# Decay rows and gate rows of a DeltaNet layer spread over the partitions by DMA from DRAM instead of by transpositions

## The chip, the cores and the metric

The kernel runs on one core of one Trainium2 chip. The metric is the device time of one launch in microseconds (us), the median of several runs. The engines are TensorE (PE; PEld is its weight load), VectorE (DVE), ScalarE (ACT), GpSimd (POOL) and SyncE (SP); each runs its own queue of instructions in order. DMAs are issued from a queue of an engine, here SP's and POOL's.

## The reference

One decoder layer on 256 rows of 2048 float32 values, with a conditioning vector c: a modulation (six vectors of 2048, among them the gates ga1 and ga2), a gated DeltaNet with 16 query/key heads and 32 value heads of 128, and a SwiGLU of width 5632, each followed by a residual sum and a layer norm.

```python
mod = (silu(c) @ mod_w + mod_b)              # sh1, sc1, ga1, sh2, sc2, ga2
h   = x * (1 + sc1) + sh1
qkv, z, b, a = split(h @ w_in)               # conv of 4 taps and silu on qkv
beta, g = sigmoid(b), -exp(a_log) * softplus(a + dt_bias)
gc    = cumsum(g)                            # within a chunk, per value head
decay = where(i >= j, exp(gc[i] - gc[j]), 0)
L     = where(i > j, beta[i] * (k[i] . k[j]) * decay, 0)
u, w  = solve(I + L, [v * beta, k * beta * exp(gc)])
o     = chunk by chunk: q*exp(gc) @ state + (where(i>=j, q.k * decay)) @ (u - w @ state)
x = layer_norm(alpha * x + ga1 * (gated_norm(o, z) @ w_out))
x = layer_norm(alpha * x + ga2 * ((silu(h2 @ w_gate) * (h2 @ w_up)) @ w_down))
```

So `gc` is used twice per head, once along the rows (a value per partition) and once along the columns of a matrix (the same row of 128 values in every partition). The gates ga1 and ga2 multiply along the columns too: the same row of 2048 values in every partition.

## The kernel before

The large matrix products (w_in, w_out, w_gate/w_up, w_down) take almost all of PE's time. Weights stream from DRAM in blocks of 512 KB (`raw`), issued by SP. ACT rounds each block to the reduced type of PE (`wh`, L190), DVE subtracts to get the rest (`wl`, L191), and each product is three matmuls (hi x wh, hi x wl, lo x wh; L223 to L225) of 128x128 by 128x512. I call these the main matmuls. `raw`, `wh` and `wl` have four buffers each, one block serves 12 main matmuls.

The work of the DeltaNet is laid between the main matmuls of w_in (and, at its end, of other products). The code is written as small generators with a due time in units of 24 main matmuls; `advance` runs those that are due as the main products are written, `at(p)` gives them that priority, and `yield d` puts the rest of a task d units later. So constants such as LA1, LA2 and LA3 set where an instruction stands among the main matmuls. The engines then run what stands in their queue, in order.

The 32 value heads are worked in four groups q of 8, one stretch of the program each. Once at the start of the DeltaNet `gates` (L410) makes beta, gc, its negative ngc and others, as columns: one value per partition (position in a chunk of 128), one column per chunk and head. In each stretch there are four tasks `la_task` (two chunks c by two halves g of four heads). A task makes `dg`, gc of four heads added to a mask `below` of -1e30 (L543, ACT, Identity with bias), transposes the four matrices on PE into a PSUM tile `gd` (L547), takes Exp of it with bias ngc into `dm` (L551, ACT), multiplies keys with keys and queries on PE into another `gd` tile `pk` (L556), and multiplies `pk` with `dm` on DVE into `LA` (L561). `gd` has two buffers in PSUM; `dg` and `dm` share the tag `V` of three buffers with tiles of `state_task`. `solve_task` then starts by reading the diagonal blocks of `LA`, and `state_task` follows (its last product is V times LA, L685). At its end come a power on POOL for the output norm (`fo`, L718), a product on DVE (L719) and the multiplication with z (L795). Inverse norms `rn` of keys and queries are POOL powers too (L509), read on DVE (`rr`).

The gate rows: `gate_row` makes, for ga1 and ga2, a tile of 128 x 2048 by 16 transposes of a column repeated 128 times (L838) and four ACT copies (L839); `residual` reads it (L845) after the first column group of w_out and of w_down.

Of the kernel before, what the change touches and what calls it, by code (L numbers as in the profile page):

```python
# [8 lines left out]
F32 = mybir.dt.float32  # L9
F32R = mybir.dt.float32r  # L10
I32 = mybir.dt.int32
AF = mybir.ActivationFunctionType
OP = mybir.AluOpType
# [3 lines left out]
D = 2048  # L17
S = 256
KT = D // 128
# [10 lines left out]
def gdn_layer_kernel(ctx: ExitStack, tc: tile.TileContext, x, c, mod_w, mod_b, ln_g, ln_b,  # L30
                     w_gu, w_down, w_in, conv_w, a_log, dt_bias, norm_w, w_out, out):
    nc = tc.nc
# [2 lines left out]
    SPLIT, MOD0, MODEVERY = 10, 30.0, 0.95  # L35
    MGAP, CGAP0, CGAP, CSTEP = 1.5, 1.0, 2.0, 2.3
    CONV, PAIR, SILU = 0.2, 0.4, 2.4
    GDN, LAGAP, LA1, LA2, LA3, SOLVE, HOP = 3.0, 0.5, 0.3, 0.6, 1.5, 5.4, 0.6
    ALONE, MACW, ZW, OW = 1.5, 1.0, 0.1, 0.3


    consts = ctx.enter_context(tc.tile_pool(name="consts", bufs=1))
    work = ctx.enter_context(tc.tile_pool(name="work", bufs=2))
# [3 lines left out]
    dram = ctx.enter_context(tc.tile_pool(name="dram", bufs=2, space=DRAM))  # L47

    act = nc.scalar.activation
    tt = nc.vector.tensor_tensor  # L50
    ts = nc.vector.tensor_scalar
    stt = nc.vector.scalar_tensor_tensor
    mm = nc.tensor.matmul
    tr = nc.tensor.transpose
# [35 lines left out]
    def tp():  # L90
        return psum.tile([128, 512], F32, name="tp", tag="tp", bufs=2)

    def gd():
        return psum.tile([128, 512], F32, name="gd", tag="gd", bufs=2)
# [17 lines left out]
    jp = work.tile([128, 128], I32, name="jp", tag="hf", bufs=2)  # L112
    nc.gpsimd.iota(jp, pattern=[[1, 128]], base=0, channel_multiplier=-1)
    ident = consts.tile([128, 128], F32, name="ident")
# [3 lines left out]
    ones = upper[:, 127:128]  # L118
    mhalf = consts.tile([128, 16], F32, name="mhalf")
    nc.vector.memset(mhalf, -0.5)  # L120
    below = consts.tile([128, 128], F32, name="below")
    ts(below, jp, 0.0, -1e30, op0=OP.is_gt, op1=OP.mult)

    pbit = work.tile([128, 1], I32, name="pbit", tag="gw0", bufs=1)
    nc.gpsimd.iota(pbit, pattern=[[0, 1]], base=0, channel_multiplier=1)
# [7 lines left out]
    p = tp()  # L133
# [16 lines left out]
    p = tp()  # L150
# [244 lines left out]
    gp = gp_ctx.__enter__()  # L395
# [6 lines left out]
    gc = consts.tile([128, 2, 32], F32, name="gc")  # L402
    ngc = consts.tile([128, 2, 32], F32, name="ngc")
    egc = consts.tile([128, 32], F32, name="egc")
    negc = consts.tile([128, 32], F32, name="negc")
    XN = gp.tile([64, 16, 64], F32, name="XN", tag="XN", bufs=1)
    nc.gpsimd.memset(XN[0:32, :, 32:64], 0.0)
    kse = consts.tile([128, 32], F32, name="kse")

    def gates(ps):  # L410
        bT = work.tile([128, 256], F32, name="bT", tag="hf", bufs=2)
        act(bT[64:128, :], ps[64:128, 0:256], AF.Copy)
        p = tp()
        for t in range(2):
            tr(p[:, t * 64:(t + 1) * 64], bT[64:128, t * 128:(t + 1) * 128], ident[64:128, 64:128])
        ba = work.tile([128, 2, 64], F32, name="ba", tag="hf", bufs=2)
        nc.vector.tensor_copy(ba, p[:, 0:128].rearrange("p (a b) -> p a b", a=2))
        nA = work.tile([128, 32], F32, name="nA", tag="gw0", bufs=1)
        act(nA, alogB, AF.Exp)
        e = work.tile([128, 2, 32], F32, name="e", tag="gw1", bufs=1)  # L420
        act(e, ba[:, :, 0:32], AF.Exp, scale=-1.0)
        ts(e, e, 1.0, None, op0=OP.add)
        nc.vector.reciprocal(beta, e)
        xa = work.tile([128, 2, 32], F32, name="xa", tag="gw2", bufs=1)
        tt(xa, ba[:, :, 32:64], dtB[:, None, :].to_broadcast([128, 2, 32]), op=OP.add)
        ab = work.tile([128, 2, 32], F32, name="ab", tag="gw3", bufs=1)
        stt(ab, xa, -1.0, xa, op0=OP.mult, op1=OP.max)
        en = work.tile([128, 2, 32], F32, name="en", tag="gw1", bufs=1)
        act(en, ab, AF.Exp, scale=-1.0)
        s = work.tile([128, 2, 32], F32, name="s", tag="gw3", bufs=1)  # L430
        ts(s, en, 2.0, None, op0=OP.add)
        nc.vector.reciprocal(s, s)
        tt(s, s, en, op=OP.mult)
        s2 = work.tile([128, 2, 32], F32, name="s2", tag="gw1", bufs=1)
        tt(s2, s, s, op=OP.mult)
        q = work.tile([128, 2, 32], F32, name="q", tag="gw4", bufs=1)
        ts(q, s2, 1.0 / 15.0, None, op0=OP.mult)
        for n in (13, 11, 9, 7, 5, 3):
            stt(q, q, 1.0 / n, s2, op0=OP.add, op1=OP.mult)
        stt(q, q, 1.0, s, op0=OP.add, op1=OP.mult)  # L440
        ts(xa, xa, 0.0, None, op0=OP.max)
        stt(q, q, 2.0, xa, op0=OP.mult, op1=OP.add)
        stt(q, q, -1.0, nA[:, None, :].to_broadcast([128, 2, 32]), op0=OP.mult, op1=OP.mult)
        p = tp()
        mm(p[:, 0:64], upper, q.rearrange("p a b -> p (a b)"), start=True, stop=True)
        mm(p[:, 64:96], ones.to_broadcast([128, 128]), q[:, 0, :], start=True, stop=True)
        nc.vector.tensor_copy(gc, p[:, 0:64].rearrange("p (a b) -> p a b", a=2))
        ts(ngc, gc, -1.0, None, op0=OP.mult)
        act(egc, gc[:, 1, :], AF.Exp)
        ts(negc, egc, -1.0, None, op0=OP.mult)  # L450
        tt(kse, p[:, 64:96], gc[:, 0, :], op=OP.subtract)
        act(kse, kse, AF.Exp)
# [83 lines left out]
    def la_task(q, c, g, sc):  # L536

        kqq, hv, la = kq[q], q * 8, LA[q]
        s0 = c * 8 + g * 4
        dg = gp.tile([128, 4, 128], F32, name="dg", tag="V", bufs=3)  # L540
        for i in range(4):
            h = hv + g * 4 + i
            act(dg[:, i, :], below, AF.Identity, bias=gc[:, c, h:h + 1])  # L543
        yield LA1
        pb = gd()
        for i in range(4):
            tr(pb[:, i * 128:(i + 1) * 128], dg[:, i, :], ident)  # L547
        dm = gp.tile([128, 4, 128], F32, name="dm", tag="V", bufs=3)
        for i in range(4):
            h = hv + g * 4 + i  # L550
            act(dm[:, i, :], pb[:, i * 128:(i + 1) * 128], AF.Exp, bias=ngc[:, c, h:h + 1])  # L551
        yield LA2
        pk = gd()
        for n in range(2):
            nn = g * 2 + n
            mm(pk[:, n * 256:(n + 1) * 256], kqq[:, nn, 0, c * 128:(c + 1) * 128],  # L556
               kqq[:, nn, :, c * 128:(c + 1) * 128], start=True, stop=True)
        for i in range(4):
            h = g * 4 + i
            src = pk[:, (i // 2) * 256:(i // 2 + 1) * 256].rearrange("p (a b) -> p a b", a=2)  # L560
            stt(la[:, s0 + i], src, sc[:, 0, c, h:h + 1], dm[:, i, None, :].to_broadcast([128, 2, 128]),  # L561
                op0=OP.mult, op1=OP.mult)
# [268 lines left out]
    def gate_row(tag, cols, name):  # L831

        row = held.tile([128, D], F32, name=name, tag=tag)
        for g in range(4):
            p = tp()
            for i in range(4):
                k = 4 * g + i
                tr(p[:, i * 128:(i + 1) * 128], cols[:, k:k + 1].to_broadcast([128, 128]), ident)  # L838
            act(row[:, g * 512:(g + 1) * 512], p, AF.Copy)  # L839
        return row  # L840

    def residual(row, g, t, ps, xin, st):
# [157 lines left out]
    with at(n0 + 16):  # L1000
        for src, op in ((ln_g, OP.mult), (ln_b, OP.add)):
            row = held.tile([128, D], F32, name="lrow", tag="h2")
# [16 lines left out]
    with tc.tile_pool(name="ph3", bufs=1, reuse_waits="tile") as p3:  # L1019
# [67 lines left out]
        for g in range(4):  # L1087
            if g == 1:
                for i, src in enumerate((ln_g, ln_b)):
                    for gg in range(4):  # L1090
                        tag, n = ("sg", 2) if i and gg > 1 else ("an", 6)
# [32 lines left out]
```

## Time and profile before

| what | value |
|---|---|
| median of 3 runs | 1725.81 us (1724.95 to 1726.1) |
| profiled execution | 1724.8 us, its span 1723.0 us, mean PE clock 0.992 |
| busy PE, PEld | 1668.4 us (97%), 1325.3 us (77%) |
| busy DVE, ACT, POOL | 1140.0 us (66%), 879.3 us (51%), 49.0 us (3%) |
| chain that ended last | PE 71%, DVE 11%, DMA 8%, issue 5%, ACT 3% |

The span is the time from the first to the last instruction of the profiled execution. The chain is the work that ended last, followed back to what released each step. The mean duration of an instruction includes time in which its predecessor still runs in the pipeline; the step between two starts is the cost on a full engine.

### The profile page before, as it was taken

Reading aid. Unit: us, or ns where it says so; the run is one execution under the profiler, and the core shown is the slowest. Engines: PE = TensorE matmul, PEld = TensorE weight load, DVE = VectorE, ACT = ScalarE, POOL = GpSimd, SP = SyncE. Lnnn points to the kernel's source line nnn. Section 1 sums busy time; section 2 is a strip of 40 time slices with the busy share of each in tenths; the row PEclk is TensorE's granted clock in tenths of the full one; section 3 lists DMA queues with packets and bytes.
Section 4 is the critical chain, followed back from the end, with each engine's and each line's share of the span. In section 5 each row is a group of like instructions: output and inputs, shape, how many; then the busy total and the mean of one; then the engine's idle time right before and its main releaser. Section 6 shows DMA issues by size and latency. Waiting matters only on the chain.

```text
span 1723.0 us, 23257 instructions
## 1 busy us (share of the span) xinstructions
PE 1668.4 (97%) x8685; PEld 1325.3 (77%) x8685; DVE 1140.0 (66%) x1641; ACT 879.3 (51%) x1426; POOL 49.0 (3%) x58
## 2 busy tenths in 40 slices
PE   5999999999999999999999999999999999999996
PEld 2666777787887878787788778888878887888885
DVE  2466988958966988847776865764567444455455
ACT  2433669769568667564333734444444443433331
POOL 0000000001001000000000000000000000000000
PEclk8999999999999999999999999999999999999998
DMA  9998785535863777747888576886678666765653
GB/s 351 364 337 282 225 290 186 171 111 160 257 205 112 245 247 240 247 147 237 300 285 278 159 259 193 298 271 188 187 243 290 186 190 204 249 195 190 196 193 107
DMA packets 183938, 390.82 MB, mean 227 GB/s; under 512 B 12096, under 2 KB 14320, under 8 KB 182800
## 3 DMA queue, kind: packets, MB, share of 16 engines
q1 hardware_dynamic: 181808, 378.64, 67.5%
q0 software_dynamic: 2016, 10.68, 1.8%
q8 instruction: 68, 1.11, 0.3%
q14 instruction: 46, 0.38, 0.1%
HBM read 385.08 MB, written 4.19 MB: 226 GB/s over the span
## 4 chain that ended last, share of the span: by engine, by line
PE 71%; DVE 11%; DMA 8%; issue 5%; ACT 3%; POOL 1%; SPq 1%; DVEq 0%; POOLq 0%; ACTq 0%
PE pj L224 19%; PE pj L223 19%; PE pj L225 19%; DMA mraw<-in_mod_w_dram 6%; DVE wl L191 5%; DVE macc L272 1%; PE gd L225 1%; PE gd L224 1%; ACT wh L190 1%; PE gd L223 1%; PE tp L311 1%; DVE X L586 1%; DVE cy L470 1%; DVE tmp L584 1%; PE tp L1039 1%
## 5 line engine op out<-in xcount | busy, mean ns | idle before, releaser
L191 DVE TENSOR_TENSOR wl<-raw,wh 128x1024 fp32r<-128x1024 f32 x522 | 634.9, 1222 | 375.5 <-ACT wh L190 372.4
L190 ACT ACTIVATE wh<-raw 128x1024 fp32r<-128x1024 f32 x522 | 552.3, 1061 | 603.2 <-PE pj L225 480.9
L223 PE MATMUL pj<-wh,h2T 128*128 128x512 f32 x704 | 278.2, 395 | 0.0
L225 PE MATMUL pj<-wh,h2T 128*128 128x512 f32 x704 | 276.7, 393 | 0.0
L224 PE MATMUL pj<-wl,h2T 128*128 128x512 f32 x704 | 276.6, 393 | 0.0
L223 PE MATMUL pj<-wh,hT 128*128 128x512 f32 x640 | 256.9, 403 | 0.0
L224 PE MATMUL pj<-wl,hT 128*128 128x512 f32 x640 | 256.4, 401 | 0.1
L225 PE MATMUL pj<-wh,hT 128*128 128x512 f32 x640 | 256.2, 401 | 0.0
L272 DVE SCALAR_TENSOR_TENSOR macc<-mraw,cond,macc 128x1024 f32<-128x1024 f32 x120 | 153.4, 1278 | 55.8 <-DMA mraw<-in_mod_w_dram 55.4
L223 PEld LDWEIGHTS pj<-wh,h2T 128*128 128x128 f32 x704 | 132.8, 189 | 30.7 <-issue 1.6
L225 PEld LDWEIGHTS pj<-wh,h2T 128*128 128x128 f32 x704 | 132.7, 189 | 28.6 <-issue 0.8
L224 PEld LDWEIGHTS pj<-wl,h2T 128*128 128x128 f32 x704 | 132.7, 188 | 27.5 <-issue 0.8
L223 PEld LDWEIGHTS pj<-wh,hT 128*128 128x128 f32 x640 | 120.8, 189 | 26.6 <-issue 3.3
L225 PEld LDWEIGHTS pj<-wh,hT 128*128 128x128 f32 x640 | 120.9, 189 | 24.6 <-issue 1.2
L224 PEld LDWEIGHTS pj<-wl,hT 128*128 128x128 f32 x640 | 120.8, 189 | 24.4 <-DVE wl L191 0.9
L470 DVE SCALAR_TENSOR_TENSOR cy<-tp,cw,cy 128x255 f32<-128x255 f32 (+2 forms) x192 | 86.2, 476 | 1.3 <-ACT cy L466 1.2
L224 PE MATMUL gd<-wl,hT 128*128 128x512 f32 x128 | 51.5, 404 | 1.4 <-DVE wl L191 1.4
L223 PE MATMUL gd<-wh,hT 128*128 128x512 f32 x128 | 49.9, 398 | 2.0 <-DVE part L256 1.1
L225 PE MATMUL gd<-wh,hT 128*128 128x512 f32 x128 | 51.8, 408 | 0.0
L311 PE MATMUL tp<-mraw,cond 128*32 128x256 f32 x368 | 34.9, 464 | 11.1 <-DMA mraw<-in_mod_w_dram 11.1
L223 PE MATMUL pj<-wh,oTc 128*128 128x512 f32 x112 | 43.9, 392 | 0.0
L225 PE MATMUL pj<-wh,oTc 128*128 128x512 f32 x112 | 43.8, 391 | 0.0
(385 smaller groups left out, 2252.0 us busy)
## 6 DMA issues: line engine op xcount, KB each, us to landing
raw<-in_gdn_w_in_dram SPq DMA_DIRECT2D x194, 512.0 KB, 4.7
mraw<-in_mod_w_dram SPq DMA_DIRECT2D x192, 512.0 KB, 5.4
raw<-in_ffn_w_gu_dram SPq DMA_DIRECT2D x176, 512.0 KB, 4.4
raw<-in_ffn_w_down_dram SPq DMA_DIRECT2D x88, 512.0 KB, 4.7
raw<-in_gdn_w_out_dram SPq DMA_DIRECT2D x64, 512.0 KB, 5.0
x<-in_x_dram SPq DMA_DIRECT2D x8, 256.0 KB, 6.0
r<-in_x_dram POOLq DMA_DIRECT2D x2, 1024.0 KB, 5.1
x1s<-r POOLq DMA_DIRECT2D x2, 1024.0 KB, 6.7
```

Of the source, the lines that this page charges most:

```text
L190: act(hi, raw, AF.Copy)
L191: tt(lo, raw, f32(hi), op=OP.subtract)
L223: mm(ps, sh, wh, start=start, stop=False)
L224: mm(ps, sh, wl, start=False, stop=False)
L225: mm(ps, sl, wh, start=False, stop=stop)
L272: return stt(acc, w, cond[:, k:k + 1], acc, op0=OP.mult, op1=OP.add)
L311: mm(p[32 * j:32 * j + 32, 0:hw], cond[:, k:k + 1].to_broadcast([128, 32]), raw[:, kl, j * hw:(j + 1) * hw], start=(k == 0), stop=(k == KT ...
L470: stt(y[:, o + s:o + 256], p[:, o:o + 256 - s], tap(3 - s, ct + i), y[:, o + s:o + 256], op0=OP.mult, op1=OP.add)
L584: tt(tv, LD[:, j + 1:32, j:j + 1].to_broadcast([128, n, m]), X[:, j, None, 0:m].to_broadcast([128, n, m]), op=OP.mult)
L586: tt(X[:, j + 1:32, 0:m], X[:, j + 1:32, 0:m], tv, op=OP.subtract)
L1039: tr(p[:, i * 256 + t * 128:i * 256 + (t + 1) * 128], nats[j, t][:, (2 * i2 + i) * 128:(2 * i2 + i + 1) * 128], ident)
```

## The change

In `gates` gc is transposed once (64 rows of 128), copied by DVE and written to a scratch `gcrows` in DRAM. Each `la_task` then reads its four rows from there into all 128 partitions (256 KB, POOL's queue), and POOL sets the part above the diagonal to -1e30 by an affine_select; Exp works in place. `dg`, `below` and the PSUM tile of the transposes are gone. LA1 is 1.6 for 0.3 and LA3 2.8 for 1.5. In `gate_row` the columns are transposed once, copied, written to DRAM and read back into all partitions.

```diff
--- before.py
+++ after.py
@@ -35,7 +35,7 @@
     SPLIT, MOD0, MODEVERY = 10, 30.0, 0.95
     MGAP, CGAP0, CGAP, CSTEP = 1.5, 1.0, 2.0, 2.3
     CONV, PAIR, SILU = 0.2, 0.4, 2.4
-    GDN, LAGAP, LA1, LA2, LA3, SOLVE, HOP = 3.0, 0.5, 0.3, 0.6, 1.5, 5.4, 0.6
+    GDN, LAGAP, LA1, LA2, LA3, SOLVE, HOP = 3.0, 0.5, 1.6, 0.6, 2.8, 5.4, 0.6
     ALONE, MACW, ZW, OW = 1.5, 1.0, 0.1, 0.3
 
 
@@ -118,8 +118,6 @@
     ones = upper[:, 127:128]
     mhalf = consts.tile([128, 16], F32, name="mhalf")
     nc.vector.memset(mhalf, -0.5)
-    below = consts.tile([128, 128], F32, name="below")
-    ts(below, jp, 0.0, -1e30, op0=OP.is_gt, op1=OP.mult)
 
     pbit = work.tile([128, 1], I32, name="pbit", tag="gw0", bufs=1)
     nc.gpsimd.iota(pbit, pattern=[[0, 1]], base=0, channel_multiplier=1)
@@ -403,6 +401,7 @@
     ngc = consts.tile([128, 2, 32], F32, name="ngc")
     egc = consts.tile([128, 32], F32, name="egc")
     negc = consts.tile([128, 32], F32, name="negc")
+    gcrows = dram.tile([64, 128], F32, name="gcrows", tag="gcrows", bufs=1)
     XN = gp.tile([64, 16, 64], F32, name="XN", tag="XN", bufs=1)
     nc.gpsimd.memset(XN[0:32, :, 32:64], 0.0)
     kse = consts.tile([128, 32], F32, name="kse")
@@ -446,6 +445,12 @@
         mm(p[:, 64:96], ones.to_broadcast([128, 128]), q[:, 0, :], start=True, stop=True)
         nc.vector.tensor_copy(gc, p[:, 0:64].rearrange("p (a b) -> p a b", a=2))
         ts(ngc, gc, -1.0, None, op0=OP.mult)
+
+        pr = tp()
+        tr(pr[:64, 0:128], gc.rearrange("p a b -> p (a b)"), ident)
+        gr = work.tile([64, 128], F32, name="gr", tag="hf", bufs=2)
+        nc.vector.tensor_copy(gr, pr[:64, 0:128])
+        nc.gpsimd.dma_start(gcrows, gr)
         act(egc, gc[:, 1, :], AF.Exp)
         ts(negc, egc, -1.0, None, op0=OP.mult)
         tt(kse, p[:, 64:96], gc[:, 0, :], op=OP.subtract)
@@ -537,18 +542,15 @@
 
         kqq, hv, la = kq[q], q * 8, LA[q]
         s0 = c * 8 + g * 4
-        dg = gp.tile([128, 4, 128], F32, name="dg", tag="V", bufs=3)
+        dm = gp.tile([128, 4, 128], F32, name="dm", tag="V", bufs=3)
+        h0 = c * 32 + hv + g * 4
+        nc.gpsimd.dma_start(dm, gcrows[None, h0:h0 + 4, :].to_broadcast([128, 4, 128]))
+        nc.gpsimd.affine_select(dm, dm, pattern=[[0, 4], [1, 128]], compare_op=OP.is_ge, fill=-1e30,
+                                base=0, channel_multiplier=-1)
+        yield LA1
         for i in range(4):
             h = hv + g * 4 + i
-            act(dg[:, i, :], below, AF.Identity, bias=gc[:, c, h:h + 1])
-        yield LA1
-        pb = gd()
-        for i in range(4):
-            tr(pb[:, i * 128:(i + 1) * 128], dg[:, i, :], ident)
-        dm = gp.tile([128, 4, 128], F32, name="dm", tag="V", bufs=3)
-        for i in range(4):
-            h = hv + g * 4 + i
-            act(dm[:, i, :], pb[:, i * 128:(i + 1) * 128], AF.Exp, bias=ngc[:, c, h:h + 1])
+            act(dm[:, i, :], dm[:, i, :], AF.Exp, bias=ngc[:, c, h:h + 1])
         yield LA2
         pk = gd()
         for n in range(2):
@@ -831,12 +833,13 @@
     def gate_row(tag, cols, name):
 
         row = held.tile([128, D], F32, name=name, tag=tag)
-        for g in range(4):
-            p = tp()
-            for i in range(4):
-                k = 4 * g + i
-                tr(p[:, i * 128:(i + 1) * 128], cols[:, k:k + 1].to_broadcast([128, 128]), ident)
-            act(row[:, g * 512:(g + 1) * 512], p, AF.Copy)
+        p = tp()
+        tr(p[:KT, 0:128], cols, ident)
+        rows = work.tile([KT, 128], F32, name="grow", tag="rows", bufs=2)
+        nc.vector.tensor_copy(rows, p[:KT, 0:128])
+        there = dram.tile([KT, 128], F32, name=f"{name}d", tag=name, bufs=1)
+        nc.gpsimd.dma_start(there, rows)
+        nc.gpsimd.dma_start(row, there.rearrange("k p -> (k p)")[None, :].to_broadcast([128, D]))
         return row
 
     def residual(row, g, t, ps, xin, st):
```

Three places of the order follow, from the second stretch (q of 1). The first is PE, around the last product of the state of the stretch before (`V2` by `LA`). Before:

```order
L685 MATMUL gd_3248<-V2_3208,LA_2086 128x128 x4
L224 MATMUL pj_3442<-wl_3792,hT01_117 128x512
L225 MATMUL pj_3442<-wh_3791,hT11_119 128x512
L223 MATMUL pj_3443<-wh_3785,hT01_117 128x512
L224 MATMUL pj_3443<-wl_3786,hT01_117 128x512
L547 MATMUL gd_3329<-ident_78,dg_3305 128x128
L225 MATMUL pj_3443<-wh_3785,hT11_119 128x512
L547 MATMUL gd_3329<-ident_78,dg_3305 128x128
```

After:

```order
L222 MATMUL pj_3355<-wl_3509,hT01_115 128x512
L223 MATMUL pj_3355<-wh_3508,hT11_117 128x512
L687 MATMUL gd_3280<-V2_3236,LA_2090 128x128 x4
L558 MATMUL gd_3490<-kq_2028 128x256 x2
L221 MATMUL pj_3356<-wh_3508,hT01_115 128x512
L222 MATMUL pj_3356<-wl_3509,hT01_115 128x512
L558 MATMUL gd_3566<-kq_2028 128x256 x2
L499 MATMUL tp_3522<-ident_78,kq_3297 128x128 x4
L223 MATMUL pj_3356<-wh_3508,hT11_117 128x512
```

The transposes of line 547 are gone, and the products of the first two tasks (`gd_3490`, `gd_3566`) stand right behind the state's last; those of the third task stand 28 main matmuls later.

The second is POOL, the whole of the stretch; `dm` are the decay tiles of the four tasks, `fo0` the power of the output norm, `rn` the inverse norms. Before:

```order
L576 MEMSET X_3589 128x512
L578 COPY X_3589<-parity_89 128x16 x2
L718 TENSOR_TENSOR fo0_3258<-ft_3259,mhalf_82 128x16
L509 TENSOR_TENSOR rn_3551<-ss_3058,mhalf_82 128x8
L509 TENSOR_TENSOR rn_3812<-ss_3441,mhalf_82 128x8
```

After:

```order
L547 DMA dm_3337<-gcrows_126 128x512
L547 DMA dm_3395<-gcrows_126 128x512
L547 DMA dm_3429<-gcrows_126 128x512
L720 TENSOR_TENSOR fo0_3290<-ft_3291,mhalf_82 128x16
L548 AFFINE_SELECT dm_3337<-dm_3337 128x512
L548 AFFINE_SELECT dm_3395<-dm_3395 128x512
L548 AFFINE_SELECT dm_3429<-dm_3429 128x512
L547 DMA dm_3459<-gcrows_126 128x512
L548 AFFINE_SELECT dm_3459<-dm_3459 128x512
L514 TENSOR_TENSOR rn_3536<-ss_3008,mhalf_82 128x8
L514 TENSOR_TENSOR rn_3654<-ss_3354,mhalf_82 128x8
```

Eight instructions come in; `fo0` stands behind three transfers and ahead of the selects, `rn` behind the fourth select.

The third is DVE, at the products of the four tasks into `LA`. Before:

```order
L561 SCALAR_TENSOR_TENSOR LA_3300<-gd_3382,gsc_3301,dm_3334 128x256 x4
L191 TENSOR_TENSOR wl_3951<-raw_3948,wh_3950 128x1024
L561 SCALAR_TENSOR_TENSOR LA_3300<-gd_3420,gsc_3301,dm_3374 128x256 x4
L191 TENSOR_TENSOR wl_4038<-raw_4035,wh_4037 128x1024
L561 SCALAR_TENSOR_TENSOR LA_3300<-gd_3487,gsc_3301,dm_3412 128x256 x4
L507 TENSOR_SCALAR ss_3058<-ss_3058 128x8
L561 SCALAR_TENSOR_TENSOR LA_3300<-gd_3543,gsc_3301,dm_3464 128x256 x4
L512 TENSOR_SCALAR rr_3553<-rn_3551 128x16
```

After:

```order
L563 SCALAR_TENSOR_TENSOR LA_3332<-gd_3490,gsc_3333,dm_3337 128x256 x4
L189 TENSOR_TENSOR wl_3862<-raw_3859,wh_3861 128x1024
L563 SCALAR_TENSOR_TENSOR LA_3332<-gd_3566,gsc_3333,dm_3395 128x256
L189 TENSOR_TENSOR wl_3868<-raw_3865,wh_3867 128x1024
L563 SCALAR_TENSOR_TENSOR LA_3332<-gd_3566,gsc_3333,dm_3395 128x256
L512 TENSOR_SCALAR ss_3008<-ss_3008 128x8
L563 SCALAR_TENSOR_TENSOR LA_3332<-gd_3566,gsc_3333,dm_3395 128x256
L517 TENSOR_SCALAR rr_3538<-rn_3536 128x16
L353 SCALAR_TENSOR_TENSOR ga1_112<-tp_3552,modb_97 128x8
L521 TENSOR_TENSOR ik_3540<-rr_3538,ss_3008 128x16
L563 SCALAR_TENSOR_TENSOR LA_3332<-gd_3566,gsc_3333,dm_3395 128x256
```

The last product of the second task (`gd_3566`) now stands behind `rr`, which reads `rn`.

## Rows read from the trace of the kernel before

**Rows 1.** The page, parts 1 and 4: busy time by engine, and the chain.
```profile
PE 1668.4 (97%) x8685; PEld 1325.3 (77%) x8685; DVE 1140.0 (66%) x1641; ACT 879.3 (51%) x1426; POOL 49.0 (3%) x58
...
PE 71%; DVE 11%; DMA 8%; issue 5%; ACT 3%; POOL 1%; SPq 1%; DVEq 0%; POOLq 0%; ACTq 0%
```

**Rows 2.** The waits: who waits, for whom, total us, times, longest us.
```profile
ACT wh L190 <- PE pj L225: 480.9, 334, 5.7
```

**Rows 3.** The windows: length, busy time (count) by engine, clock, DMA share, GB/s.
```profile
500.00:550.00 50.00, 49.97 (x263) 40.77 (x262) 26.65 (x49) 42.35 (x124) 4.54 (x2) 1.00 0.32 95
```

**Rows 4.** PE's timeline at 540 us: start, duration, engine, line, operation, out<-in.
```profile
540.27 0.39 PE L225 MATMUL pj<-wh,hT 128*128 128x512 f32 x1
540.50 1.02 PE L556 MATMUL gd<-kq 128*128 128x256 f32 x4
...
541.59 0.40 PE L224 MATMUL pj<-wl,hT 128*128 128x512 f32 x1
```

**Rows 5.** PE's timeline at 251 us: four transpositions in a row.
```profile
250.88 0.39 PE L225 MATMUL pj<-wh,hT 128*128 128x512 f32 x1
251.11 0.60 PE L547 MATMUL gd<-ident,dg 128*128 128x128 f32 x4
...
251.78 0.40 PE L224 MATMUL pj<-wl,hT 128*128 128x512 f32 x1
```

**Rows 6.** The instructions of line 838: ns min/median/max, first to last start.
```profile
L838 PE MATMUL tp<-ident,ga x32: 271/272/323, 790.7 to 1473.1; 128*128 128x128 f32 x32
```

**Rows 7.** PE's timeline at 662 us.
```profile
662.15 0.67 PE L556 MATMUL gd<-kq 128*128 128x256 f32 x2 [0.92 <-DVE LA L561]
```

**Rows 8.** POOL queue's DMAs over the span: count, KB, median us to landing.
```profile
x1s<-r POOLq DMA_DIRECT2D x2, 1024.0 KB, 6.7
...
l<-in_ln_b_dram POOLq DMA_DIRECT2D x4, 256.0 KB, 8.6
...
prow<-in_ln_g_dram POOLq DMA_DIRECT2D x1, 16.0 KB, 4.5
```

**Rows 9.** The instructions of line 845, where the gate rows are read first.
```profile
L845 DVE TENSOR_TENSOR ry<-pj,ga1row x8: 680/684/691, 819.5 to 958.0; 128x512 f32<-128x512 f32 x8
L845 DVE TENSOR_TENSOR ry<-pj,ga2row x8: 683/688/693, 1526.0 to 1709.3; 128x512 f32<-128x512 f32 x8
```

**Rows 10.** PE's timeline at 390 us: the last product of a state.
```profile
390.69 1.05 PE L685 MATMUL gd<-V,LA 128*128 128x128 f32 x8
```

**Rows 11.** POOL queue's DMAs from 1460 to 1464.5 us: 256 KB alone.
```profile
l<-in_ln_b_dram POOLq DMA_DIRECT2D x1, 256.0 KB, 3.9
```

**Rows 12.** POOL's timeline at 253, 304, 395 and 618 us.
```profile
252.98 0.53 POOL L576 MEMSET X<- 128x512 f32 x1 [3.50 <-PE tp L462]
253.57 0.34 POOL L578 COPY X<-parity 128x16 f32<-128x16 f32 x2
...
303.63 1.64 POOL L509 TENSOR_TENSOR rn<-ss,mhalf 128x8 f32<-128x8 f32 x1 [49.71 <-DVE ss L507]
...
394.73 2.90 POOL L718 TENSOR_TENSOR fo<-ft,mhalf 128x16 f32<-128x16 f32 x1 [34.19 <-DVE ft L717]
...
617.83 1.57 POOL L578 COPY X<-parity 128x16 f32<-128x16 f32 x2
```

**Rows 13.** The groups by form: busy us and mean ns of one, idle before.
```profile
L561 DVE SCALAR_TENSOR_TENSOR LA<-gd,gsc,dm 128x256 f32<-128x256 f32 x64 | 26.5, 476 | 5.1 <-PE gd L556 3.4 <-PE gd L547 1.2 <-ACT wh L190 0.6
...
L551 ACT ACTIVATE dm<-gd,ngc 128x128 f32<-128x128 f32 x64 | 19.0, 372 | 1.1 <-PE gd L547 1.0
```

**Rows 14.** DVE's timeline from 397 us.
```profile
397.66 0.17 DVE L719 TENSOR_TENSOR fo<-fo,rr 128x16 f32<-128x16 f32 x1
...
397.87 2.19 DVE L795 SCALAR_TENSOR_TENSOR oq<-oq,fo,nat 128x128 f32<-128x128 f32 x8
399.98 1.22 DVE L191 TENSOR_TENSOR wl<-raw,wh 128x1024 fp32r<-128x1024 f32 x1
```

**Rows 15.** DVE's timeline at 618 us.
```profile
617.79 1.27 DVE L272 SCALAR_TENSOR_TENSOR macc<-mraw,cond,macc 128x1024 f32<-128x1024 f32 x1
```

## The prediction

> **What bounds the kernel now.** I read the page first: TensorE (PE) is busy for 1668.4 of 1723.0 us and holds 71% of the chain that ended last, VectorE (DVE) 11%, the transfers 8% [rows 1]. Then the waits: ScalarE (ACT) waits 480.9 us for PE, in 334 places, with its next copy of a weight block [rows 2]; so ACT runs ahead of PE and stands still because PE has not released a weight buffer. Third the windows: in one of the four stretches where the changed work lies PE is busy for 49.97 of 50 us, at full clock [rows 3]. The reader is to see that an instruction on PE's queue costs its own length there, that one less on ACT or DVE gives nothing, and that a new wait in PE's queue costs its whole length, since the queue is in order.
>
> **What goes.** Transposes of the decay rows: between two main matmuls around the four of line 547 the way from 250.88 to 251.78 is 0.90 us where two plain steps of 0.23 (540.27 to 540.50 [rows 4]) take 0.46, so four cost 0.44 us, 0.11 each [rows 5]. That is the lower end. For one alone between main matmuls, no row is clean; a main matmul's record lasts 0.39 at a step of 0.23 and a transposition's 0.272 [rows 6], in the same proportion 0.16: the upper end. There are 64: 7.0 to 10.2 us; I take 0.14, so 9.0, since in three of the four stretches most stand singly. Transposes of the gate rows: 32 [rows 6], by the same 0.11 each 3.5 us; three new ones (two for the gate rows, one for gc) cost 0.3, no gain elsewhere, so 3.2; most stand alone, up to 4.6, and I take 3.4. One stall of 0.92 us is also seen in the last stretch, where a product waits for a PSUM buffer of line 561 with the transposes in between [rows 7]; the transposes no longer use that PSUM pair, so I count it as gone: 1.0 (bounds 0 and 1). Sum of what goes: 9.0 + 3.4 + 1.0 = 13.4 us, between 10.2 (7.0 + 3.2) and 15.8 (10.2 + 4.6 + 1.0).
>
> ACT loses 64 additions and 8 copies; by its wait for PE [rows 2] that is worth nothing. The `below` mask is one DVE instruction before the steady part: nothing.
>
> **What comes, off the path.** The gate rows go through two transfers each. The nearest rows are 6.7 us for 1 MB to DRAM and 4.5 for a small one [rows 8]: some 12 us with the issues. The old transposes ended at 790.7 and 1473.1 [rows 6]; the rows are read first at 819.5 and 1526.0 [rows 9]. So 29 and 53 us of other work cover them; without that cover they would cost those 12 us each. The write of gcrows is paid once, in the first of the four stretches (below).
>
> **What comes, on the path.** The four products of line 558 per stretch (call them g1 to g4) use two PSUM buffers; g3's can't start until g1's four DVE products of line 563 have read the first buffer, g4's not before g2's. Those need the decay tile: transfer, POOL select, Exp. In the order after, g1 and g2 stand right behind the last product of the state, L687, and g3 28, 31 and 37 main matmuls later in the second, third and fourth stretch, g4 10, 7 and 4 after g3. I count from T0, the end of that last product (391.74 before [rows 10]). Prices: a transfer 4.2 us (3.9 alone [rows 11], 4.5 the small one [rows 8]); a select 0.8 (no row has one; the MEMSET of its shape takes 0.53 [rows 12], and a read beside the write can only add to it; 1.57 for the COPY is the other end, below); the pow of `fo` 2.9, of `rn` 1.64 [rows 12]; four Exp 1.2 (19.0/16) and four DVE products 1.66 (26.5/16) [rows 13]; `fo`'s product 0.2, eight z products 2.2 and a weight remainder 1.22 [rows 14]; one group of products on PE 0.86 (from 540.27 to 541.59 is 1.32, less two steps [rows 4]).
>
> Second stretch. POOL runs three transfers, then `fo`, then three selects. pow starts 3.0 after T0 (394.73 [rows 12]) and ends at 5.9, the selects by 8.3, the first one's Exp at 7.9. DVE: fo's product, eight z products and a remainder, 5.9 + 0.2 + 2.2 + 1.2 = 9.5, then g1's four, 11.2. PE has done g1, g2 (1.7), 28 steps (6.4) and four transposes (0.5) by 8.6: a wait of 2.6. Then g4: the fourth transfer is issued only when g1's tile is free, at 11.2; it lands at 15.4, select 16.2, and behind it on POOL is `rn`, until 17.9; `rr`, which needs it, stands on DVE ahead of g2's last product, so that ends at 18.9. PE is there at 11.2 + 0.9 + 2.3 + 1.5 = 15.9 (14 transposes and sums between): 3.0 more. Third stretch: first select 5.0, a transfer issue 5.5, `fo` 8.4, then 0.2, a remainder and four products, 11.5; PE at 1.7 + 0.5 + 7.1 = 9.3: 2.2. Fourth: second select 6.3, `fo` 9.2, two remainders and four products, 13.5; PE at 1.7 + 8.4 = 10.1: about 3.3. First: no state is before it, but the gcrows write (4.5), a transfer (4.2) and a select lie ahead of `rn`, and DVE falls about 4 us behind; I take 2.5, the mean of g3's waits in the others, bounds 0 and 5. Sum 2.6 + 3.0 + 2.2 + 3.3 + 2.5 = 13.6.
>
> Queued behind PE's wait are main matmuls; ACT and DVE then fill all four weight buffers, no more (the lead is at most 48 steps, 11 us), so nothing is caught up later. Below, this sum falls to some 2 us where DVE runs `fo`'s chain earlier or PE comes later than I count (each of five waits is the difference of two numbers near 10); above, to 25, where selects take 1.57 and the transfers 8.6, as the queued ones of the same size do [rows 8].
>
> The 256 KB transfer took 3.9 us alone [rows 11]. The Trainium skill (DMA: Bandwidth & Descriptors, Anatomy of one DMA, the SWDGE path) has a fit of 2.0 us plus the bytes over 436e3, which is 2.6 us for this one; the measurement is longer and decides. By the fit, an estimate, the first selects would come 1.6 us sooner in the third and fourth stretch and g4's in the second: three waits of that much, near 5 us less.
>
> **The sum.** 1724.8 (the profiled execution, 1.0 below the median of the three) - 13.4 + 13.6 = 1725.0; on the median's scale 1726. What PE no longer does it waits for.
>
> **Rivals.** *The waits don't bite.* If the products of line 563 come before PE reaches g3 and g4, only the removal is left: 1725.8 - 13.4 = 1712.4, with 1 us for the shorter waits 1713. For it: the due time of the products is put off (LA1, LA3), and ACT and DVE have spare time. Against: the pow of `fo` in front of the selects, and z products ahead of g1's on DVE, both read from the order.
>
> *POOL is held by DVE (slower).* The COPY of line 578 takes 0.34 us at 253.57 but 1.57 at 617.83, while a DVE product with two SBUF inputs runs from 617.79 for 1.27 [rows 12, 15]; `wl`, 1.22 us [rows 14], has two SBUF inputs too. If each select on a chain is held for such an instruction, it takes some 1.1 us more; with two or three on the chain of each stretch that is 10 us: 1736. It decides where a select takes over 1.5 us from landing to end. The Trainium skill (SBUF - State Buffer, SBUF: two separate sides) states the rule: DVE's two-input instructions and GpSimd's reads take one port pair, an exclusive lock held by whichever began first, the other blocked. The trace agrees, once in two COPYs; by the rule nearly every select begun beside `wl` would be held, and my sum is too low. For this rival: DVE is busy for 66% [rows 1]; against: in 26.65 of 50 us only in the third stretch [rows 3], and four selects of a stretch rarely all meet one.
>
> *The transfers queue* (the 8.6 us case) is the same side and counted with it.
>
> **How the numbers follow.** A difference of 0.2%, 3.45 us, is about what a measurement of this kernel can tell from no change. Forecast, saving and waits cancel within that: 0.38, its own range 1722 to 1730. Waits don't bite or half of them: 0.32, from 1712 to 1722. Held or queued POOL: 0.30, from 1730 to 1742. The prices I can bound reach from 1725.8 - 15.8 + 2 = 1712 to 1725.8 - 10.2 + 25 = 1741; a tenth is left out on each side: 1714 to 1738. Faster 0.32, same 0.38, slower 0.30.
>
> **What would show it.** In the profile after: PE's busy time some 12 us lower but the span not; PE's idle time in front of line 558 put down to DVE's line 563, five waits of 2 to 3.5 us. No wait of PE or DVE for `ga1row` or `ga2row`. A select of 0.6 to 1.0 us after 4 us of transfer. I am wrong if line 558 has no wait over 1 us (then 1713), or if selects take 1.5 us or more, or transfers 6 us, and line 558 waits over 4 us each time (then 1736). A wait of ACT's copies for POOL's selects, which stand ahead of them in ACT's queue through Exp, would be a cost I have at nothing, because ACT is ahead of PE by up to 11 us.

## The result, and the profile after

The changed kernel takes 1745.83 us (median of 4 runs, 1743.35 to 1746.63), the kernel before 1725.95 (median of 4, 1724.95 to 1727.91): 1.0111 times as long, 95% interval [1.0094, 1.0129]. It is 19.9 us slower and outside the predicted range of 1714 to 1738. One run of the early loads below (1854.16 us) and one of the kernel before that ran beside it (2082.79 us) had a lower granted clock throughout, 0.851 and 0.751, and count in no median or ratio here. The profiled execution has a span of 1744.7 us, 21.7 more than before.

The page after, the lines that answer to [rows 1]:

```profile
PE 1664.5 (95%) x8592; PEld 1321.6 (76%) x8592; DVE 1147.1 (66%) x1643; ACT 863.1 (49%) x1358; POOL 70.9 (4%) x95
...
PE 60%; DVE 16%; DMA 11%; issue 7%; ACT 4%; POOL 2%; SPq 1%; DVEq 0%; POOLq 0%; ACTq 0%
```

PE's busy time fell by only 3.9 us and the rest of the span, in which PE stands, grew from 54.6 to 80.2, by 25.6. PE's share of the chain fell from 71% to 60%. Mean granted clock is 0.986, before 0.992: by these rounded means some 24 us of full clock missing against 14, the start and the end of the span included.

The waits after: who waits, for whom, total us, times, longest us.

```profile
POOL dm L548 <- DMA dm<-gcrows: 28.8, 8, 4.4
...
DVE rr L517 <- POOL rn L514: 18.3, 8, 4.0
...
PE gd L558 <- DVE LA L563: 13.5, 3, 6.3
...
DVE fo L721 <- POOL fo L720: 11.1, 3, 4.3
...
PE tp L534 <- ACT cy L478: 5.1, 3, 2.5
...
PE tp L534 <- DVE cy L475: 4.1, 2, 3.3
```

Two lines answer for these waits in the kernel before:

```profile
DVE fo L719 <- POOL fo L718: 5.1, 3, 3.0
...
DVE rr L512 <- POOL rn L509: 4.4, 4, 1.4
```

PE's wait before the products of line 558 is the forecast one (13.5 us, forecast 13.6). The reader is to see the rest of the list too: DVE's wait for `rn` went from 4.4 to 18.3 us, POOL's selects wait 28.8 us for transfers, and PE waits 9.2 us before line 534, the transposes of the convolved values `cy`, where I had no wait at all.

The chain of the first stretch, in order of time (start, duration, what):

```profile
246.60 0.55 POOL dm L547
...
251.11 0.65 POOL dm L548
251.75 1.67 POOL rn L514
...
253.44 0.03 DVE rr L517
...
256.76 1.25 DVE cy L475 x4
```

A transfer issued at 246.60 holds the select until 251.11, the select holds `rn`, `rn` holds DVE at `rr`, the products of `cy` behind it come late, and PE waits 3.32 us at 258.86. PE's timeline goes on:

```profile
258.86 0.63 PE L534 MATMUL tp<-ident,cy 128*128 128x128 f32 x4 [3.32 <-DVE cy L475]
...
260.41 0.63 PE L221 MATMUL pj<-wh,hT 128*128 128x512 f32 x1
260.83 0.63 PE L222 MATMUL pj<-wl,hT 128*128 128x512 f32 x1
```

A step of 0.42 us from 260.41 to 260.83, where 0.23 is usual: the lower of the two clocks, 1.2 GHz. The windows show it (length, busy time and count of PE, PEld, DVE, ACT, POOL, then granted clock, DMA share, GB/s):

```profile
260.00:270.00 10.00, 10.00 (x42) 8.05 (x41) 8.34 (x13) 7.99 (x14) 0.00 (x0) 0.83 0.84 271
400.00:410.00 10.00, 5.64 (x20) 4.36 (x19) 9.38 (x19) 6.33 (x23) 2.97 (x5) 0.84 0.25 68
540.00:550.00 10.00, 7.16 (x26) 5.58 (x25) 6.98 (x14) 7.49 (x28) 4.76 (x5) 0.84 0.47 145
590.00:600.00 10.00, 7.45 (x29) 5.79 (x28) 9.31 (x24) 4.42 (x10) 0.00 (x0) 0.83 0.75 250
690.00:700.00 10.00, 6.43 (x21) 5.29 (x22) 8.23 (x16) 5.31 (x8) 2.31 (x2) 0.66 0.45 131
...
690.16:693.57 3.41, 0.00 (x0) 0.03 (x1) 3.41 (x6) 2.59 (x5) 0.00 (x0) 0.50 0.37 80
```

From 260 to 270 PE is busy all the time and has 0.83 of its clock. Each of the five waits over 2.5 us in this trace between 240 and 720 us (3.32, 4.36, 2.84, 2.55 and 6.31) is followed by such a stretch. The five windows miss 1.7, 1.6, 1.6, 1.7 and 3.4 us of clock, 10.0 in all; the kernel before has full clock from 240 to 720 us. Where the clock falls within a wait that part costs nothing: from 690.16 to 693.57 PE stands, at 0.50 of its clock (the last line). While PE works it has 0.50 in the five places for 3.4, 2.8, 3.1, 3.4 and 3.4 us, 16.2 in all, so some 8 us are lost. The 769th main matmul starts at 276.6, before at 269.7: 6.9 us later, of which 3.3 are the wait and 1.7 the clock (0.17 of 10 us); part of the rest is work of this stretch that now stands earlier, and at the 961st the lag is 4.5 us.

The second stretch, POOL's timeline:

```profile
397.64 2.95 POOL L720 TENSOR_TENSOR fo<-ft,mhalf 128x16 f32<-128x16 f32 x1
400.55 1.81 POOL L548 TENSOR_SCALAR_AFFINE_SELECT dm<-dm 128x512 f32<-128x512 f32 x3
```

DVE's timeline there, and PE's:

```profile
400.62 1.77 DVE L721 TENSOR_TENSOR fo<-fo,rr 128x16 f32<-128x16 f32 x1 [3.41 <-POOL fo L720]
...
405.67 1.65 DVE L563 SCALAR_TENSOR_TENSOR LA<-gd,gsc,dm 128x256 f32<-128x256 f32 x4
```

```profile
407.47 2.04 PE L558 MATMUL gd<-kq 128*128 128x256 f32 x4 [4.36 <-DVE LA L563]
```

The chain is the forecast one, power, selects, z products, then line 563, and PE at its place (403.1, about 8.5 us after the state's last product, forecast 8.6). But `fo`'s product took 1.77 us where it took 0.17 before [rows 14]: it begins with the three selects, from 400.55 to 402.36, and ends with them. In the third and fourth stretch it starts with a select too, and takes 0.60 us each time; at the end, with no select beside it (795.57), 0.17. So the port was taken the other way round than in [rows 12, 15], POOL first and DVE blocked; this is what the Trainium skill (SBUF - State Buffer, SBUF: two separate sides) says of whichever starts first, and I had drawn only one half of it.

The prices (instructions of line 548; transfers, median us to landing):

```profile
L548 POOL TENSOR_SCALAR_AFFINE_SELECT dm<-dm x16: 625/636/1711, 251.1 to 698.0; 128x512 f32<-128x512 f32 x16
```

```profile
dm<-gcrows POOLq DMA_DIRECT2D x16, 256.0 KB, 4.4
```

A select takes 0.64 us (forecast 0.8), two of the sixteen over 1.5, at most 1.71; a transfer 4.4 (forecast 4.2). Line 848, which reads the gate rows, waits for PE alone; the rows land 14 and 38 us before it first reads them.

### The profile page after: what moved, and what is told of

It reads as the page before. It is cut to its first block, busy times and chain, and to the rows that moved or that the text cites. A ratio compares the mean times of both kernels' runs of the same rounds, so it can differ in the third digit from the quotient of the medians.

```text
span 1744.7 us, 23052 instructions
## 1 busy us (share of the span) xinstructions
PE 1664.5 (95%) x8592; PEld 1321.6 (76%) x8592; DVE 1147.1 (66%) x1643; ACT 863.1 (49%) x1358; POOL 70.9 (4%) x95
## 4 chain that ended last, share of the span: by engine, by line
PE 60%; DVE 16%; DMA 11%; issue 7%; ACT 4%; POOL 2%; SPq 1%; DVEq 0%; POOLq 0%; ACTq 0%
PE pj L221 16%; PE pj L222 16%; PE pj L223 16%; DMA mraw<-in_mod_w_dram 8%; DVE wl L189 6%; DVE macc L270 2%; ACT wh L188 1%; DVE cy L475 1%; DVE X L588 1%; DVE tmp L586 1%; PE gd L223 1%; DMA dm<-gcrows 1%; PE gd L222 1%; PE gd L221 1%; POOL rn L514 1%
## 5 line engine op out<-in xcount | busy, mean ns | idle before, releaser
L222 PE MATMUL pj<-wl,oTc 128*128 128x512 f32 x112 | 43.9, 392 | 0.3 <-DVE wl L189 0.3
L221 PE MATMUL pj<-wh,oTc 128*128 128x512 f32 x112 | 43.9, 392 | 0.0
```

The costliest lines, as they stand in the source:

```text
L221: mm(ps, sh, wh, start=start, stop=False)
L222: mm(ps, sh, wl, start=False, stop=False)
```

## The experiments

Each ratio is to runs of the kernel before made beside it on the same chip, with its 95% interval. Kernels told together were not all run together, so they are compared by these ratios.

**One part at a time.** The first takes the new `gate_row` into the kernel before, the second the old one into the changed kernel (the function as in the diff, all else unchanged).

> The kernel before with the new gate_row alone (decay rows as before, LA1 and LA3 as before). Theory A (PE's in-order waits behind the POOL queue in the decay part, and the lower clock after each long wait, make the whole loss): the gate rows are covered by 29 and 53 us of other work, 30 transpositions less, 1722.5 us (1720 to 1724.5). Rival B (the added traffic through the scratch disturbs the weight stream): two broadcasts of 1 MB cost something, 1726 to 1730.

Measured: 1720.01 us, ratio 0.9962 [0.995, 0.9974].

> The changed kernel with the old gate_row. Theory A: the whole loss is here, 1745.8 + 3.4 = 1749 us (1746 to 1752). Rival B: part of the loss came from the gate rows' transfers, 1740 to 1745.

Measured: 1749.55 us, ratio 1.0141 [1.0116, 1.0166]. By the ratios the gate rows alone gain 6.6 us (4.5 to 8.6), more than the 3.4 of their transpositions; the decay rows alone lose 24. So traffic (rival B) is out for the gate rows, which move 1 MB at a time; for the transfers of the decay rows the third kernel of the next group bounds it.

**What stands on POOL's queue.** Four kernels take away the selects, the powers, or both (the last from the kernel before with the new gate rows), and so leave out parts of the computation.

```diff
-        nc.gpsimd.affine_select(dm, dm, ...)                       # no select
-            act(dm[:, i, :], dm[:, i, :], AF.Exp, bias=ngc[...])
+            act(dm[:, i, :], dm[:, i, :], AF.Exp, bias=gc[...])

-        nc.gpsimd.tensor_tensor(r..., ss..., mhalf[:, 0:8], op=OP.pow)   # no powers
+        ts(r, ss, 0.0, 0.15, op0=OP.mult, op1=OP.add)
-        nc.gpsimd.tensor_tensor(f..., t..., mhalf, op=OP.pow)
+        ts(f, t, 0.0, 1.0, op0=OP.mult, op1=OP.add)
```

> The changed kernel without the affine_select (the part above the diagonal isn't masked, and Exp takes gc as bias so that values stay small). Theory A1 (POOL's selects, which wait for the landing of a transfer, hold the powers rn and fo behind them, DVE waits for those, and PE for DVE): the 7 us lost in the first stretch go and some of the others, 1736 us (1731 to 1740). Rival A2 (the landing itself, 4.4 us behind a late tile, is what line 558 waits for): 1742 to 1746.

Measured: 1733.96 us, ratio 1.0049 [1.0032, 1.0066]. In its trace DVE no longer waits at the place of the chain above; `rr` follows its power. DVE's waits for all the powers fell from 29.4 to 23.0 us only (the second and third line):

```profile
248.54 0.17 DVE L517 TENSOR_SCALAR rr<-rn 128x16 f32<-128x16 f32 x1 [0.41 <-POOL rn L514]
...
DVE fo L719 <- POOL fo L718: 13.0, 4, 3.4
DVE rr L517 <- POOL rn L514: 10.0, 8, 1.6
```

Here every `rn` but one (1.1 us) starts within 0.3 us of its input and every `fo` within 0.5, so hardly anything on POOL holds them; yet DVE's wait for them was 9.5 us in the kernel before, and PE waits 8.1 before the same products (line 556 here). In the second stretch of the kernel before two weight remainders stand on DVE between `fo`'s input and its product; in this kernel nothing does. PE's waits before line 534 fell from 9.2 to 2.5 us.

> The changed kernel with the powers rn and fo replaced by a DVE instruction of their shape that writes a constant (the norms aren't computed). Theory A1 (selects that wait for a landing, and the powers, stand in one queue and hold each other): nothing is held behind a select any more but other selects, and fo no longer stands ahead of the selects; the 7 us of the first stretch go and the waits of line 558 lose up to 2.9 each, 1728 us (1722 to 1735). Rival A2 (landing late because the tiles come free late): 1738 to 1746.

Measured: 1725.88 us, ratio 1.0001 [0.9987, 1.0014]. The wait of PE before the same products (line 557 here) fell from 13.5 to 1.8 us, though its selects still wait for transfers, longer than in the changed kernel:

```profile
POOL dm L547 <- DMA dm<-gcrows: 35.3, 13, 4.8
...
PE gd L557 <- DVE LA L562: 1.8, 3, 0.9
```

With no power behind them, selects that wait for longer cost PE little at these products.

> The changed kernel without the affine_select (no mask, gc as Exp's bias) and with the powers rn and fo replaced by a DVE instruction that writes a constant: only transfers are left on POOL in the stretches. Theory A1 (selects and powers cost because they stand in one queue): taking away one of them was enough, this one is near the kernel without powers, 1720 to 1726 us. Rival A2 (each costs for itself: the selects by ACT's wait, the powers by DVE's): the gains of 12 and 20 us add up, 1711 to 1716.

Measured: 1718.97 us, ratio 0.9963 [0.9946, 0.9979].

> A control for the two kernels without powers: the kernel before with the new gate_row, decay rows by transpositions, and the powers rn and fo replaced by a DVE instruction that writes a constant. Theory A1 (a power costs only where a select that waits for a landing stands in its queue): the same as with the powers, 1720 us (1716 to 1721). Rival (DVE's waits for the powers are worth as much in the kernel before): 1700 to 1712, and then most of the 20 us gained without powers says nothing on the change.

Measured: 1717.11 us, ratio 0.9949 [0.9933, 0.9966]. By the ratios times 1725.8, powers are worth 0.0013, 2 us, in a kernel without transfers for the decay rows, and 0.0110, 19 us, in the changed one. Together, as the loss of the new decay rows against the old, both with the new gate rows (each field is known to some 4 us either way):

| | powers on POOL | no powers |
|---|---|---|
| selects | 1.0111 - 0.9962: 25.7 us | 1.0001 - 0.9949: 9.0 us |
| no selects | 1.0049 - 0.9962: 15.0 us | 0.9963 - 0.9949: 2.4 us |

Taking away the selects gains 10.7 us, the powers 16.7, both 23.3. So the two mostly add up; what they cost only together, held behind each other in one queue, is 4.1 us, and by the intervals (6 either way) it can be none. The 1719.0 of the kernel without either lies 1 us under A1's range and 3 us over A2's; that one of the two was enough (A1) it does not bear out, as it is 6 us below the kernel without powers. The last field is within the intervals of its two ratios: with nothing but transfers on POOL the new decay rows are level with 64 transpositions, no faster, and their traffic costs no more than a few us. Its trace shows a longer standing of PE in place of the transpositions. The windows from the 577th to the 2305th main matmul, without either and then with transpositions and no powers:

```profile
218.00:762.40 544.40, 528.64 (x3301) 426.26 (x3299) 434.38 (x865) 376.35 (x778) 16.82 (x31) 1.00 0.66 209
...
217.90:764.60 546.70, 539.19 (x3396) 435.50 (x3395) 434.93 (x870) 391.74 (x853) 5.53 (x13) 1.00 0.64 200
```

PE stands for 15.8 us there (544.40 less 528.64) against 7.5. The busy times do not compare: 32 small products of the first kernel come behind the window.

**Earlier transfers.** Here the tiles of a stretch lie in the buffers of the solve (X, diag, LD), and their transfers and selects are issued when the solve before ends. A second kernel does so without selects; a third is the changed kernel with the old LA1 and LA3.

```diff
+    def dm_load(q, c, g):
+        ...                          # dm in the tags X, diag, LD
+        nc.gpsimd.dma_start(dm, gcrows[...])
+        yield LSEL
+        nc.gpsimd.affine_select(dm, dm, ...)
...
         yield from solve_task(q)
+        if q < NQ - 1:
+            dm_loads(q + 1)
```

> The changed kernel with the transfers and selects of a stretch issued at the end of the solve before it, into the buffers of the solve that are free then (no more the three buffers shared with the state), LA1 0.3 and LA3 1.5 as before. Theory A: waits of line 558 over 1 us go, no low clock after them, 1713 us (1709 to 1719). Rival B (traffic) or rival C (what was gained by removing transpositions isn't on PE's path): 1735 and more with the same transfers, or 1722 to 1727 with no waits.

Measured: 1745.71 us, ratio 1.011 [1.0086, 1.0134]. A miss by over 30 us. It lies in rival B's range, but what traffic can cost is bounded above. PE still waits before the products, less, and new waits came:

```profile
POOL dm L557 <- DMA dm<-gcrows: 50.6, 13, 7.0
...
ACT dm L573 <- POOL dm L557: 12.2, 7, 3.3
...
DVE fo L743 <- POOL fo L742: 9.0, 4, 3.1
...
PE gd L578 <- DVE LA L583: 6.6, 3, 2.3
```

The products' wait halved (6.6 for 13.5 us), but they now stand behind `fo`'s wait alone, which I had not removed; and ACT, whose queue holds the state's copies too, waits 12.2 us for selects that wait 50.6 us for transfers. The head of the queue was only put elsewhere. The lower clock takes more here too: behind waits of 1.91 and 1.58 us in the solve PE, busy with small products, has 0.66 of its clock for 15 us, twice:

```profile
510.00:525.00 15.00, 15.00 (x90) 12.45 (x89) 4.92 (x5) 7.99 (x17) 3.33 (x5) 0.66 0.52 169
640.00:655.00 15.00, 14.41 (x85) 12.33 (x84) 8.58 (x15) 7.90 (x19) 3.58 (x5) 0.66 0.72 231
```

That is 5 us each.

> The kernel of the early loads without the affine_select (part above the diagonal not masked, Exp with gc as bias). Theory A1: what the early loads lost again is ACT's and DVE's wait for the selects and for the powers behind them; without selects 1722 us (1715 to 1730). Rival A3 (the early loads lose by holding the buffers of the solve, X, diag and LD): 1738 to 1747.

Measured: 1739.34 us, ratio 1.009 [1.0069, 1.011]. Without selects it is 6 us better by the medians and 3.5 by the ratios, which is within their intervals; A1 had 24. Theory A1 fell for the early loads, and A3's range holds. Whether it is the held buffers, the late `fo` or the lower clock was not separated.

> The changed kernel with LA1 0.3 and LA3 1.5 as before the change. Theory A (waits of PE behind the POOL queue, and the low clock after them): the products of line 558 and the solve are due earlier, the transfers land no sooner, so the waits are as long or longer, 1746 to 1756 us. Rival C (the later due times themselves cost the time, by packing the solve between other work): 1730 to 1740.

Measured: 1748.96 us, ratio 1.0134 [1.0117, 1.0151]. The new due times are not what costs; without them it is no better.

**A wait by itself.** The kernel before, with six blocks of the gate/up weights held back by memsets of their buffer on POOL.

```diff
+            for _ in range(HOLD.get(len(blocks), 0)):    # {270: 6, 300: 8, ... 420: 16}
+                nc.gpsimd.memset(raw, 0.0)
             nc.sync.dma_start(raw.rearrange("p (a b) -> p a b", a=a), src)
```

> The kernel before, with six weight blocks of the gate/up product held back by 6, 8, 10, 12, 14 and 16 memsets of their buffer on POOL ahead of the load (the values are loaded after). This measures a wait of PE by itself. Theory A (clock): PE waits of some 1, 3, 5, 7, 9 and 11 us; after those over 2.5 us the granted clock stands at 1.2 GHz for 3 to 4 us, so each costs its length and 1.5 to 2 us more. Rival (the lower clock comes from the mix of small matmuls in the DeltaNet, not from a wait): steps of 0.23 us straight after each wait.

Measured: 1743.17 us (two runs), ratio 1.0104 [1.0082, 1.0126]. The graded row of waits did not come out; most holds were covered, and two single waits over 2.5 us stand among main matmuls, in a part with no small products of the solve. PE's timeline after the first, and after the second:

```profile
1111.33 1.41 PE L1043 MATMUL tp<-ident,an 128*128 128x128 f32 x6 [3.29 <-DVE an L1035]
...
1113.39 0.63 PE L227 MATMUL pj<-wh,h2T 128*128 128x512 f32 x1
1113.82 0.63 PE L228 MATMUL pj<-wl,h2T 128*128 128x512 f32 x1
```

```profile
1354.08 1.22 PE L227 MATMUL pj<-wh,h2T 128*128 128x512 f32 x2 [4.32 <-ACT wh L194]
...
1355.93 0.63 PE L229 MATMUL pj<-wh,h2T 128*128 128x512 f32 x1
```

The windows around them:

```profile
1100.00:1108.00 8.00, 8.00 (x37) 6.21 (x35) 3.89 (x4) 3.07 (x3) 0.00 (x0) 1.00 0.84 291
...
1112.00:1116.00 4.00, 4.00 (x15) 3.31 (x14) 4.00 (x5) 1.50 (x3) 0.00 (x0) 0.63 0.94 292
1116.00:1124.00 8.00, 8.00 (x37) 6.61 (x36) 6.16 (x5) 3.00 (x4) 0.00 (x0) 1.00 0.83 291
...
1354.00:1361.00 7.00, 6.89 (x16) 4.96 (x17) 4.63 (x4) 3.86 (x5) 0.00 (x0) 0.52 0.65 207
1361.00:1370.00 9.00, 9.00 (x42) 7.42 (x41) 4.00 (x4) 4.20 (x6) 0.00 (x0) 1.00 0.61 191
```

Against the same main matmuls of the kernel before, the first costs 5.0 us for a wait of 3.29, the second 7.9 for 4.32. The mechanism is shown apart from the DeltaNet: behind a long wait PE runs on at 1.2 GHz for a few us, here 1.5 (0.37 of 4) and 3.4 us (0.48 of 7) of lost clock. Behind the second wait stand main matmuls alone, so the rival, small products, is out as the only cause; that they add to it, as the windows of the early loads suggest, is not tested. Nor does every such wait do it: in the same trace one of 2.89 us before 966.04 is followed by full clock, one of 1.11 in the solve, before 727.21, by the lower.

**The powers elsewhere.** The complete computation with the powers on ACT (Ln, then Exp), in the changed kernel and, as a control, in the kernel before with the new gate rows.

```diff
-        nc.gpsimd.tensor_tensor(r..., ss..., mhalf[:, 0:8], op=OP.pow)
+        act(r, ss, AF.Ln)
+        act(r, r, AF.Exp, scale=-0.5)
...
-        nc.gpsimd.tensor_tensor(f..., t..., mhalf, op=OP.pow)
+        act(f, t, AF.Ln)
+        act(f, f, AF.Exp, scale=-0.5)
```

> The changed kernel, complete, with the powers rn and fo taken by ACT (Ln, then Exp with -0.5) and the selects alone on POOL. Theory A1: the gain of taking the powers off POOL is kept but for ACT's table loads, 1729 us (1724 to 1736). Rival (the gain came from DVE not waiting for any power): ACT's chain is as late as POOL's was, 1738 to 1746.

Measured: 1747.91 us, ratio 1.0135 [1.0113, 1.0157].

> A control: the kernel before with the new gate_row, and the powers on ACT too, with no decay transfers. Theory A1: powers alone on POOL wait for nothing, so moving them is worth nothing, 1720 us (1718 to 1724). Rival (the powers' own 1.6 and 2.9 us are what is gained): 1712 to 1717.

Measured: 1739.15 us, ratio 1.0081 [1.0052, 1.0109]. The move itself costs 0.0119, some 20 us. That its table loads on ACT make this cost is likely, not tested (second kernel, groups by form: busy us, mean ns):

```profile
L509 ACT ACT_TABLE_LOAD x8 | 10.3, 1283 | 0.1
L510 ACT ACT_TABLE_LOAD x8 | 10.3, 1283 | 0.1
...
L718 ACT ACT_TABLE_LOAD x4 | 5.1, 1283 | 0.1
```

Both missed what I expected. Their difference, though, 1.0135 - 1.0081, 9.3 us (some 3 to 16 by the intervals), agrees with the field of the table with selects and no powers: with the powers off POOL's queue the new decay rows are some 9 us behind in both ways of making them.

## Why the prediction was wrong

**What PE no longer does.** 13.4 us forecast. The decay rows' part of it (9.0) can be read from the windows from the 577th to the 2305th main matmul, before and after:

```profile
217.70:765.90 548.20, 538.28 (x3395) 434.07 (x3394) 432.60 (x860) 392.55 (x855) 27.66 (x23) 1.00 0.63 200
...
217.60:791.80 574.20, 539.26 (x3340) 435.29 (x3339) 441.90 (x863) 382.65 (x802) 47.30 (x56) 0.98 0.63 198
```

PE is busy 1.0 us longer, with some 8 lost to the lower clock, so the work in the window got some 7 us shorter; as eight small products more lie in the second window, some 8 have gone, within the forecast (7.0 to 10.2). The gate rows were worth more (6.6 us against 3.4, by the ratio). The cover of the rows' transfers was enough, no wait, though one figure was misread: 790.7 is where the first of the old transposes starts, the last for ga1 ends at 794.5, so the cover was 25 us and not 29.

**The waits before line 558.** Sum forecast 13.6, measured 13.5, but not place by place: 4.36, 2.84 and 6.31 in the second to fourth stretch (2.6, 2.2, 3.3 forecast), none in the first (2.5, called the mean of the others, which is 2.7) and none at g4 (3.0; there PE waits 1.54 at other transposes). That the sum fits is luck: it is no proof of its terms. The second was too small because selects block `fo`'s product on DVE (1.77 for 0.17 us).

**The step that failed** is "a new wait in PE's queue costs its whole length": I priced a wait at its own length and no more. Each of the five long ones is followed by PE at 1.2 GHz, 16.2 us of work at half the clock in all; that is some 8 us, of which the sum had none.

**The second gap** is "DVE falls about 4 us behind; I take 2.5": I saw `rn` behind the select and let DVE's lag end at g3. It ends at the next thing PE needs from DVE, `cy` at line 534: 3.32 us, 5.0 with the clock. PE's idle time grew by 25.6 us in all, 13.5 of it before line 558, 9.2 before line 534, which the sum had at nothing. The account for the stretches, by the windows above: 574.20 - 548.20 = 26.0 us longer, as PE stands 25.0 us more (34.9 against 9.9), loses some 8 to the clock and has some 7 less to do. Behind them the changed kernel makes up 4.3 us, to 21.7.

**The rivals.** "POOL is held by DVE" gave the right side and half the size (10 of 20 us) for another reason: its deciding point, selects over 1.5 us, holds for two of sixteen (median 0.64). "The waits don't bite" is refuted, and so is "The transfers queue" (4.4 us, not 8.6). A power behind a select behind a transfer, my own sentence on the first stretch, carried 2.5 us there; all that goes with the selects is 10.7 of the 25.7 us. More, 12.6 us (15.0 - 2.4), goes with powers that hardly anything holds on POOL, while DVE waits for their own length.

**What stays open:** why PE stands 8 us more in the stretches even with the transfers alone on the queue, about what leaving out the transpositions gave; and which of the causes named made the early loads lose. The version that beats both is the kernel before with the new gate rows, 1720.0 us.

## What to carry to other kernels

Before a step is moved to an idle engine, list what else stands in that engine's queue and who waits for it: a 1.6 us power behind a 4.4 us transfer costs the power's reader the transfer. Read a queue of 4% busy by its waits, not by its busy time. On a PE that is busy 97% of the span, price a wait of some us at its length plus the lower clock that can follow it (1.4 to 1.7 us here, in one case 3.4). Look also at what stands between a power and its reader: without other work there, the power's own length is a wait.

## What the runs showed of the hardware

- After waits of 3.29 and 4.32 us among otherwise steady matmuls the step was 0.43 us for 0.23 over some 3 and 6 us; after one of 2.89 us in the same trace the clock was full.
- A DVE product of 128x16 took 1.77 us beside three selects on POOL and 0.60 beside one (0.17 alone): POOL's instructions block DVE's as well as the other way round.
- An affine_select of 128x512 takes 0.64 us, a 256 KB transfer broadcast from DRAM 4.4 us. The fit of the Trainium skill (DMA: Bandwidth & Descriptors, Anatomy of one DMA) gives an estimate of 2.6; the measurement stands.
- Taken by Ln and then Exp on ACT, the eight powers `rn` cost two table loads of 1.28 us each in the kernel with transpositions; the four of `fo` cost five together.
